# Six tiles instead of four in the second block group of a down projection

## The chip, the core and the metric

The kernel runs on one core of one Trainium2 chip. The metric is the device time of one execution in microseconds (us); the time of a kernel is the median of its runs. A time is compared only with one of the same chip.

## The reference: what is computed

The reference is a two-layer encoder over 1040 positions (16 learned tokens and 1024 frames) of width 1024. Each layer has an attention part (a gated linear attention group and a softmax group side by side) and a gated feed-forward part. The change lies in the last matrix product of the feed-forward part:

```python
def conv_ffn(x, w_up, conv_w, conv_b, w_down):
    h = x @ w_up
    ...
    u, g = jnp.split(hc, 2, axis=-1)
    return (jax.nn.silu(g) * u) @ w_down
...
        h = h + conv_ffn(rms_norm(h, ffn_norm[i]), w_up[i], conv_w[i], conv_b[i], w_down[i])
```

The inner width is 2816, that is 22 tiles of 128. So `@ w_down` sums 22 tiles into 8 output tiles of 128 rows, and the residual `h` is added to each. All data are 32-bit floats.

## The kernel before, in words

**Products.** TensorE multiplies in a one-pass 32-bit form. To keep the precision each operand is split into a high part (a cast on ScalarE) and a low part (a subtraction on VectorE), and each product is three matmuls: high x high, low x high, high x low (`mm3`, L257 to L263). A matmul covers 128 inner rows and, in layer 0, 260 columns (two pieces make a half of 520); in layer 1 the first 16 positions are no longer needed, and one piece of 512 makes a half.

**Groups.** The 22 inner tiles of the down projection are worked off in five groups (L52). The tuples name a kind, the first tile and the number of tiles: three plain tiles ("n"), a block group of eight ("s"), four plain tiles ("r"), a block group of four ("s"), and at the end `LAST`, three plain tiles that run in another routine (`down_last`), chunk by chunk, with the next norm.

- A plain group computes, for each output tile m and each half, the sum over its tiles in one PSUM tile; there are four of these (`p0` to `p3`), taken in turn. Kind "n" copies the PSUM tile by ScalarE into an SBUF tile "do" (L1718), and GpSimd stores that with an accumulating DMA onto the residual in DRAM, `hm` (L1720). Three "do" tiles go round. Kind "r" reads the residual `hm` back into eight tiles `hT` first (`load_residual`, L1688 to L1691, on SP's DMA queue) and adds the PSUM tile to them on VectorE (L1716).
- A block group (`down_blocks`, L1587) takes a product of two by two blocks with seven block products instead of eight (Strassen's scheme in the variant with fifteen additions). The blocks are a pair of output tiles (j = 0 to 3), the two halves of the group's inner tiles (nk each) and the two halves of the columns. A step of `seq` is one block product p = 1 to 7 of one pair j: nk x pieces x 3 matmuls, so there are 28 steps. The weight operands (the sums A21 + A22 and so on) are built per pair by `block_operand` (VectorE, L1147) and split by `up_split` (ScalarE L1165, VectorE L1166), four steps ahead of their use. The steps build two result tiles "du" and "dg" per pair, copied on ScalarE (L1626) and added to on VectorE (L1625). When one is complete, `hand_on` either adds it to `hT` on VectorE (L1617) if the residual has been read, or stores it with an accumulating DMA (L1620). In the kernel before, the first block group stores and the second one adds.

**Column operands.** `prepare` is a generator. Step by step it reads the stored activations back (`st`, L1490 and L1496, on SP's queue), builds the seven column operands of a block group (VectorE sums L1549, splits on ScalarE L377 and VectorE L378) and splits the tiles of a plain group (L1527, L1528). It works on up to four inner tiles at a time: `k0` = 0 takes two from each half; where nk is odd, the last turn takes one from each and its operands are half as wide. `pump` (L1580) runs some steps of it after each output tile of a plain group and at some steps of a block group, as long as enough slots are free. `complete` runs it on if something is needed and not there yet.

**Slots.** All these tiles lie in 39 SBUF slots of 1040 columns (33 and 6 of the feed-forward part), handed out from a list: a slot that is given back goes to its end, the next request takes from its front. A slot is given back in program order, so its next owner may have to wait for a store that still reads it. The "do" tiles are given back at the end of the plain group; "du" and "dg", where they are stored, four steps later (`LANDING`) or at the end of the group (L1666).

**Order.** On TensorE the program order is kept as written. On the other engines a planner sets the order from the program order and its own estimates, so loads and splits can move ahead of where the code has them; each engine then works its queue strictly in order. SP only issues DMAs: weight loads (L219 for plain tiles, L1132 for blocks), activation reads and the reads of the residual.

Of the kernel before, what the change touches and what calls it, by code (L numbers as in the profile page):

```python
# [23 lines left out]
T = META + SEQ  # L24
# [24 lines left out]

GROUPS, LAST = (("n", 0, 3), ("s", 3, 8), ("r", 11, 4), ("s", 15, 4)), (19, 3)  # L52
HALVES, HALVES_LAST, HALVES_OUT = (0, 520, 520), (8, 524, 516), (16, 528, 512)
AHEAD = 4
LANDING = 4
# [115 lines left out]
class Kern:  # L171
# [1412 lines left out]
            self.need = next(self.prep)  # L1584
            n -= 1

    def down_blocks(self, lyr, g0, ng, X, pp, fw, halves, after, hT):  # L1587


        nc, s = self.nc, self.slots  # L1590
# [21 lines left out]
        going = []  # L1612

        def hand_on(i, m, x):
            if hT:
                h = hT[m][:, o0:T]
                nc.vector.tensor_tensor(out=h, in0=x[:, o0:T], in1=h, op=ALU.add)  # L1617
                s.put(x)
            else:
                nc.gpsimd.dma_start(self.hm[m][:, o0:T], x[:, o0:T], accum_op=ALU.add)  # L1620
                going.append((i + LANDING, x))
# [26 lines left out]
        def run():  # L1648
            self.among_blocks = True
            for i, (j, p) in enumerate(seq):  # L1650
                ensure(i + AHEAD)
                q = st.setdefault(j, {})
                bank, begins = {2: "y", 5: "x", 3: "x"}.get(p, "a"), p in (1, 2, 5)
                if begins:
# [23 lines left out]
    def ffn_down(self, lyr, pp, fw, halves, acts, X, ids):  # L1678
# [6 lines left out]
        two = lambda ap: ap.rearrange("p (a b) -> p a b", b=n)  # L1685
        hT, ahead, going = [], [], []

        def load_residual():  # L1688
            for k in range(KD):
                hT.append(s.get(F32, f"h{k}", first=ids))  # L1690
                nc.sync.dma_start(hT[k][:, o0:T], self.hm[k][:, o0:T])  # L1691

# [7 lines left out]
        def plain(kind, g0, ng, m, w, nxt):  # L1700
            if m == 0:
                complete(lambda: all(j in acts for j in range(g0, g0 + ng)))
                if kind == "r" and not hT:
                    load_residual()
            if kind == "n" and m == 0:

                going.extend(s.get(F32, "do") for _ in range(3))
            out = hT[m] if kind == "r" else going[m % 3]
            for h in range(2):
                ps = pp.tile([128, 2, 512], F32, tag=f"p{(2 * m + h) % 4}", name="down", bufs=1)  # L1710
                for k in range(ng):
                    for c in range(pieces):
                        self.mm3(ps[:, c, :n], w[k], acts[g0 + k], halves[h] + c * n, n, k == 0, k == ng - 1)
                x = two(out[:, halves[h]:halves[h] + W])
                if kind == "r":
                    nc.vector.tensor_tensor(out=x, in0=ps[:, :pieces, :n], in1=x, op=ALU.add)  # L1716
                else:
                    nc.scalar.copy(x, ps[:, :pieces, :n])  # L1718
            if kind == "n":
                nc.gpsimd.dma_start(self.hm[m][:, o0:T], out[:, o0:T], accum_op=ALU.add)  # L1720
            if m == KD - 1:
                s.put(*going)
                going.clear()
                for j in range(g0, g0 + ng):
                    s.put(*acts.pop(j))
            if not (nxt and built(nxt)):
                self.pump(2)
# [17 lines left out]
        def run():  # L1745
            blocks = None
            for i, part in enumerate(parts):
# [5 lines left out]
                if nxt:  # L1753
                    then = parts[i + 2] if i + 2 < len(parts) else []
                    blocks = self.down_blocks(lyr, *nxt, X[nxt[0]], pp, fw, halves,
                                              lambda t=then: t and len(ahead) < 2 and fetch(t), hT)
                for k, t in enumerate(part):
                    for _ in range(2):
                        if len(ahead) < k + 3:
# [2 lines left out]
                        blocks[0](2 * (k - len(part) + 2) + 1)  # L1762
                    plain(*t, ahead[k], nxt)
                ahead.clear()
            if not hT:
                load_residual()
            complete(lambda: all(j in acts for j in range(LAST[0], sum(LAST))))
            return hT

# [183 lines left out]
```

## Time and profile before

| | |
|---|---|
| median of 3 runs | 2470.44 us (2469.42 to 2472.99) |
| the profiled execution | 2467.24 us |
| its span, first to last instruction | 2465.5 us |
| mean granted TensorE clock | 0.999 |
| DMA traffic over the span | 260.39 MB, mean 106 GB/s |
| accumulating stores of plain tiles (L1720) | 16, each 520 KB (512 in layer 1) |
| reads of the residual (L1691) | 16, each 520 KB (512 in layer 1) |

A page has the busy time of each engine with its share of the span (PE is TensorE's matmuls, PEld its weight loads, DVE VectorE, ACT ScalarE, POOL GpSimd; SP issues DMAs). A window row gives, for a stretch of the span, its length, each engine's busy time with the number of instructions, the granted clock in parts of full speed, the busy share of the 16 DMA engines and their rate. A row of the timeline has the start, the duration, the engine, the line, the operation, output and inputs, and in brackets the idle time of the engine before it and what ended that. A row of a tile has the shortest, median and longest duration in ns, and the first and the last start in us. In a row of grouped lines stand the busy time in us and the mean in ns, and the idle time before. A DMA queue's row has packets, megabytes, and the share of the 16 engines' time (q0 is GpSimd's queue of accumulating and other software DMAs, q1 SP's and ScalarE's); a row of DMA issues has the count, the size of one and the median time to landing. A row of waits has the total, the number and the longest.

### The profile page before, as it was taken

How to read it: one execution, taken by the hardware profiler on the slowest of the kernel's cores; microseconds unless marked ns; L12 is line 12 of the kernel's file. 1: busy time of each engine (PE TensorE's matmuls, PEld its weight loads, DVE VectorE, ACT ScalarE, POOL GpSimd, SP SyncE). 2: the span in 40 equal slices, each digit the busy share in tenths (PEclk: the TensorE clock that was granted, in tenths of full speed). 3: DMA queues.
4: the chain of work that ended last, by engine and by line, in shares of the span. 5: the costliest groups of instructions: out<-in, count | busy, mean ns of one | idle time of the engine just before them, and what ended most of it. 6: DMA issues, size and time to landing. Idle time of an engine off the chain costs nothing.

```text
span 2465.5 us, 47317 instructions
## 1 busy us (share of the span) xinstructions
PE 2437.9 (99%) x18286; PEld 2356.3 (96%) x18286; DVE 1876.9 (76%) x3769; ACT 1318.9 (53%) x2857; POOL 384.6 (16%) x565
## 2 busy tenths in 40 slices
PE   9999999999999999999999999999999999999998
PEld 8999999999999999999999999999999999997887
DVE  8666777769988888865966666777799888887567
ACT  7346666646555555642643566665465555556433
POOL 2023433210000000100210234331100000001002
PEclk9999999999999999999999999999999999999999
DMA  4222224343322214863312222243423212247822
GB/s 135 70 84 76 59 84 132 120 133 95 121 82 74 91 66 144 198 169 124 125 41 73 76 81 74 65 149 106 153 81 108 91 65 91 94 153 172 214 68 88
DMA packets 121680, 260.39 MB, mean 106 GB/s; under 512 B 15248, under 2 KB 37008, under 8 KB 121456
## 3 DMA queue, kind: packets, MB, share of 16 engines
q1 hardware_dynamic: 96864, 182.05, 23.9%
q0 software_dynamic: 22288, 72.81, 10.6%
q8 instruction: 143, 2.34, 0.4%
q10 hardware_dynamic: 2304, 2.52, 0.3%
q14 instruction: 81, 0.66, 0.1%
HBM read 176.74 MB, written 67.80 MB: 99 GB/s over the span
## 4 chain that ended last, share of the span: by engine, by line
PE 68%; issue 16%; DVE 10%; ACT 4%; DMA 1%; POOL 0%; SPq 0%; DVEq 0%; POOLq 0%; ACTq 0%
PE mm L261 8%; PE mm L263 8%; PE mm L262 8%; PE up L262 5%; PE up L263 5%; PE up L261 5%; PE down L262 5%; PE down L263 5%; PE down L261 5%; PE av L782 3%; PE tr L756 2%; PE S L720 1%; DVE S L723 1%; PE S L721 1%; ACT P L735 1%
## 5 line engine op out<-in xcount | busy, mean ns | idle before, releaser
L262 PE MATMUL up<-x,lo 128*128 128x260 f32 x2240 | 631.7, 282 | 1.0 <-DVE lo L1166 1.0
L261 PE MATMUL up<-x,hi 128*128 128x260 f32 x2240 | 631.9, 282 | 0.1
L263 PE MATMUL up<-x,hi 128*128 128x260 f32 x2240 | 631.6, 282 | 0.0
L262 PEld LDWEIGHTS up<-x,lo 128*128 128x128 f32 x2240 | 422.0, 188 | 1.5 <-DVE lo L1166 1.4
L261 PEld LDWEIGHTS up<-x,hi 128*128 128x128 f32 x2240 | 421.7, 188 | 0.4 <-ACT hi L1165 0.3
L263 PEld LDWEIGHTS up<-x,hi 128*128 128x128 f32 x2240 | 421.8, 188 | 0.0
L1165 ACT CAST hi<-raw 128x512 fp32r<-128x512 f32 (+1 forms) x490 | 266.5, 553 | 207.6 <-PE up L263 88.7
L261 PE MATMUL mm<-xh,hi 128*128 128x348 f32 (+6 forms) x1056 | 359.8, 341 | 0.0
L1166 DVE TENSOR_TENSOR lo<-raw,hi 128x512 fp32r<-128x512 f32 (+1 forms) x490 | 288.0, 603 | 79.7 <-ACT hi L1165 79.1
L263 PE MATMUL mm<-xl,hi 128*128 128x348 f32 (+6 forms) x1056 | 339.6, 322 | 0.0
L262 PE MATMUL mm<-xh,lo 128*128 128x348 f32 (+6 forms) x1056 | 338.6, 321 | 0.0
L261 PEld LDWEIGHTS mm<-xh,hi 128*128 128x128 f32 x1056 | 199.4, 189 | 2.3 <-issue 1.4
L262 PEld LDWEIGHTS mm<-xh,lo 128*128 128x128 f32 x1056 | 199.4, 189 | 0.3
L263 PEld LDWEIGHTS mm<-xl,hi 128*128 128x128 f32 x1056 | 198.6, 188 | 0.1
L1147 DVE TENSOR_TENSOR raw<-raw,raw 128x512 f32<-128x512 f32 (+1 forms) x230 | 147.5, 651 | 29.8 <-DMA raw<-in_wd_dram 27.5
L735 ACT ACTIVATE P<-S,m 116x460 f32<-116x460 f32 (+2 forms) x224 | 125.1, 562 | 77.5 <-DVE m L723 74.5
L228 ACT CAST hi<-raw 128x512 fp32r<-128x512 f32 (+2 forms) x152 | 87.4, 576 | 139.6 <-PE mm L263 56.2
L262 PE MATMUL down<-x,lo 128*128 128x260 f32 (+1 forms) x504 | 161.2, 320 | 0.2 <-DVE lo L1166 0.2
L263 PE MATMUL down<-x,hi 128*128 128x260 f32 (+1 forms) x504 | 161.0, 320 | 0.0
L261 PE MATMUL down<-x,hi 128*128 128x260 f32 (+1 forms) x504 | 161.0, 319 | 0.0
L378 DVE TENSOR_TENSOR PT<-tr,PT 116x464 fp32r<-116x464 f32 (+3 forms) x240 | 123.3, 516 | 48.9 <-ACT PT L377 47.2
L1427 POOL DMA_DIRECT2D actd<-cv x44 | 23.6, 537 | 734.6 <-DVE cv L1426 734.6
(313 smaller groups left out, 5957.4 us busy)
## 6 DMA issues: line engine op xcount, KB each, us to landing
raw<-in_wm_dram SPq DMA_DIRECT2D x326, 256.0 KB, 3.1
raw<-in_wd_dram SPq DMA_DIRECT2D x48, 256.0 KB, 4.2
actd<-cv POOLq DMA_DIRECT2D x22, 520.0 KB, 3.0
actd<-cv POOLq DMA_DIRECT2D x22, 512.0 KB, 3.0
cb<-cd SPq DMA_DIRECT2D x16, 520.0 KB, 3.8
kA<-kA SPq DMA_DIRECT2D x24, 260.0 KB, 4.1
kL<-kL SPq DMA_DIRECT2D x24, 260.0 KB, 4.7
st<-actd SPq DMA_DIRECT2D x24, 260.0 KB, 3.8
```

Source lines behind the costliest of these rows:

```text
L228: nc.scalar.copy(hi[:, :n, :], raw[:, :n, :])
L261: nc.tensor.matmul(ps, wh, xh[:, c0:c0 + n], start=first, stop=False, skip_group_check=more)
L262: nc.tensor.matmul(ps, wl, xh[:, c0:c0 + n], start=False, stop=False, skip_group_check=more)
L263: nc.tensor.matmul(ps, wh, xl[:, c0:c0 + n], start=False, stop=last, skip_group_check=more)
L378: nc.vector.tensor_tensor(out=lo, in0=src, in1=hi.bitcast(F32), op=ALU.subtract)
L720: nc.tensor.matmul(S[:rows, :n], q["qA"][e][:, qs], q["kA"][e][:, c0:k1], start=True, stop=False)
L735: nc.scalar.activation(P[:rows, :n], S[:rows, :n], AF.Exp, scale=-1.0, bias=m[:rows, nch - 1:nch], accum_out=(den if nch == 1 else d3[:row ...
L756: nc.tensor.transpose(tr[:w, 3 - j, :rows], P[:rows, o:o + w], id_)
L782: nc.tensor.matmul(av[:, a:b], w.rearrange("p a b -> p (a b)"), x, start=(t == ts[0] and part == 0 and i == 0), stop=(t == last and i == 1))
L1147: nc.vector.tensor_tensor(out=q[out][:, :nk, :], in0=q[a][:, :nk, :], in1=q[b][:, :nk, :], op=op)
L1165: nc.scalar.copy(hi[:, :nk, :], src[:, :nk, :])
L1166: nc.vector.tensor_tensor(out=lo[:, :nk, :], in0=src[:, :nk, :], in1=hi[:, :nk, :].bitcast(F32), op=ALU.subtract)
```

## The change

The four plain tiles and the block group of four become two plain tiles and a block group of six (nk = 3). The two plain tiles are of kind "n": ScalarE copies them out and GpSimd stores them with accumulating DMAs; kind "r" is gone. They use five "do" tiles in turn instead of three. The residual is no longer read ahead of the plain tiles, but inside the second block group, two tiles at each of the steps 1 to 4; `hand_on` then adds to them as before. The diff, without the lines that only hand the new argument through:

```diff
-GROUPS, LAST = (("n", 0, 3), ("s", 3, 8), ("r", 11, 4), ("s", 15, 4)), (19, 3)
+GROUPS, LAST = (("n", 0, 3), ("s", 3, 8), ("n", 11, 2), ("s", 13, 6)), (19, 3)
...
         def hand_on(i, m, x):
-            if hT:
-                h = hT[m][:, o0:T]
+            if residual:
+                h = residual[0][m][:, o0:T]
                 nc.vector.tensor_tensor(out=h, in0=x[:, o0:T], in1=h, op=ALU.add)
...
             for i, (j, p) in enumerate(seq):
                 ensure(i + AHEAD)
+                if residual and 1 <= i <= KD // 2:
+                    residual[1]((2 * i - 2, 2 * i - 1))
...
-        def load_residual():
-            for k in range(KD):
+        def load_residual(ks=range(KD)):
+            for k in ks:
                 hT.append(s.get(F32, f"h{k}", first=ids))
                 nc.sync.dma_start(hT[k][:, o0:T], self.hm[k][:, o0:T])
...
         def plain(kind, g0, ng, m, w, nxt):
             if m == 0:
                 complete(lambda: all(j in acts for j in range(g0, g0 + ng)))
-                if kind == "r" and not hT:
-                    load_residual()
             if kind == "n" and m == 0:
 
-                going.extend(s.get(F32, "do") for _ in range(3))
-            out = hT[m] if kind == "r" else going[m % 3]
+                going.extend(s.get(F32, "do") for _ in range(3 if ng > 2 else 5))
+            out = going[m % len(going)]
...
-                x = two(out[:, halves[h]:halves[h] + W])
-                if kind == "r":
-                    nc.vector.tensor_tensor(out=x, in0=ps[:, :pieces, :n], in1=x, op=ALU.add)
-                else:
-                    nc.scalar.copy(x, ps[:, :pieces, :n])
-            if kind == "n":
-                nc.gpsimd.dma_start(self.hm[m][:, o0:T], out[:, o0:T], accum_op=ALU.add)
+                nc.scalar.copy(two(out[:, halves[h]:halves[h] + W]), ps[:, :pieces, :n])
+            nc.gpsimd.dma_start(self.hm[m][:, o0:T], out[:, o0:T], accum_op=ALU.add)
...
                     blocks = self.down_blocks(lyr, *nxt, X[nxt[0]], pp, fw, halves,
-                                              lambda t=then: t and len(ahead) < 2 and fetch(t), hT)
+                                              lambda t=then: t and len(ahead) < 2 and fetch(t),
+                                              None if then else (hT, load_residual))
...
-            if not hT:
-                load_residual()
```

2 lines of the change are left out of this document (1 added, 1 removed).

## The prediction

> **What bounds the kernel now.** I read the page first, then one table of windows cut at the eight stages of the two down projections, then TensorE's waits, then the rows around the end of the first block group. The page says that TensorE is never free:
>
> ```profile
> span 2465.5 us, 47317 instructions
> PE 2437.9 (99%) x18286; PEld 2356.3 (96%) x18286; DVE 1876.9 (76%) x3769; ACT 1318.9 (53%) x2857; POOL 384.6 (16%) x565
> ```
>
> The windows are, for each layer, plain tiles 0 to 2, block group 3 to 10, plain tiles 11 to 14, block group 15 to 18:
>
> ```profile
> core 0: us, PE busy (x) PEld busy (x) DVE busy (x) ACT busy (x) POOL busy (x), PEclk, DMA share, GB/s
> 998.20:1032.70 34.50, 34.50 (x290) 34.50 (x289) 33.48 (x38) 27.86 (x40) 6.55 (x8) 1.00 0.83 177
> 1032.70:1113.30 80.60, 80.60 (x674) 80.60 (x673) 48.23 (x65) 34.02 (x53) 6.81 (x8) 1.00 0.72 193
> 1113.30:1159.60 46.30, 46.30 (x387) 46.30 (x386) 20.15 (x35) 6.45 (x12) 0.85 (x1) 1.00 0.40 118
> 1159.60:1199.80 40.20, 40.20 (x338) 40.20 (x337) 32.10 (x58) 22.29 (x48) 0.00 (x0) 1.00 0.20 57
> 2220.90:2255.40 34.50, 33.67 (x146) 27.00 (x145) 30.84 (x34) 26.70 (x39) 6.56 (x8) 1.00 0.80 178
> 2255.40:2333.80 78.40, 78.20 (x337) 63.00 (x336) 48.92 (x67) 34.48 (x54) 6.83 (x8) 1.00 0.74 194
> 2333.80:2378.30 44.50, 44.50 (x194) 36.01 (x193) 20.32 (x35) 5.89 (x11) 0.86 (x1) 1.00 0.41 122
> 2378.30:2417.20 38.90, 38.90 (x170) 31.54 (x169) 31.91 (x58) 22.16 (x48) 0.00 (x0) 1.00 0.20 55
> ```
>
> In the stages that change (third and fourth row of each layer) TensorE is busy for the whole window at clock 1.00. The others are not: VectorE has 20 of 46 us, ScalarE 6. And TensorE's list of waits has only these two in the whole down projection:
>
> ```profile
> PE down L261 <- ACT do L1718: 0.8, 1, 0.8
> PE down L262 <- DVE lo L1166: 0.2, 1, 0.2
> ```
>
> So the stages end when the matmuls end, and the change is worth its matmuls, less any new wait of TensorE.
>
> **Matmuls.** The code gives the counts (a window also catches two or three at its edges). A plain tile costs 8 outputs x 2 halves x 2 pieces x 3 = 96 matmuls in layer 0 and 48, twice as wide, in layer 1. A block group of 2 nk tiles costs 28 products x nk x 2 x 3 in layer 0, half in layer 1: 336 for nk = 2, 504 for nk = 3. The change removes two plain tiles and adds 168 block matmuls: 192 - 168 in layer 0, 96 - 84 in layer 1. Rates: plain 46.30/384 = 0.1206 us and block 40.20/336 = 0.1196 in layer 0; 44.50/192 = 0.2318 and 38.90/168 = 0.2315 in layer 1. Layer 0: 192 x 0.1206 - 168 x 0.1196 = 3.1 us less. Layer 1: 96 x 0.2318 - 84 x 0.2315 = 2.8 less. If the new nk = 3 products ran at the rate of the large group (80.60/672 = 0.1199, 78.40/336 = 0.2333) it would be 3.0 and 2.65. I take 5.7 for both.
>
> **Evacuation of the plain tiles.** From the queries on the tile "down" and on the operands:
>
> ```profile
> L1718 ACT COPY do<-down x32: 565/588/605, 1003.2 to 2256.7; 128x520 f32<-128x520 f32 x16, 128x512 f32<-128x512 f32 x16
> L1716 DVE TENSOR_TENSOR h<-down,h x32: 681/693/700, 1116.8 to 2378.5; 128x520 f32<-128x520 f32 x16, 128x512 f32<-128x512 f32 x16
> L377 ACT CAST x<-st x6: 1061/1063/1065, 1096.3 to 1120.6; 128x1040 fp32r<-128x1040 f32 x6
> L378 DVE TENSOR_TENSOR x<-st,x x6: 1231/1234/1243, 1100.5 to 1123.8; 128x1040 fp32r<-128x1040 f32 x6
> L1166 DVE TENSOR_TENSOR lo<-raw,hi 128x256 fp32r<-128x256 f32 x6 | 2.3, 416 | 0.0
> L228 ACT CAST wl<-raw 128x384 fp32r<-128x384 f32 x8 | 3.8, 520 | 0.9 <-PE down L262 0.9
> L230 DVE TENSOR_TENSOR wl<-raw,wl 128x384 fp32r<-128x384 f32 x5 | 2.7, 552 | 0.5 <-ACT wl L228 0.5
> ```
>
> Per layer 16 additions leave VectorE (16 x 0.693 = 11.1 us) and 16 copies come to ScalarE (16 x 0.588 = 9.4 us). The plain stage shrinks to 192 x 0.1206 = 23.1 us, one half-tile per 1.45 us. In it ScalarE has the 9.4 us, some two whole and seven half casts of block operands (2 x 1.06 + 7 x 0.6 = 6.3, the half cast taken from the copy of the same width), 8 weight casts (8 x 0.41, as L1166 of that width) and 4 of the next group (4 x 0.52): 21.1 of 23.1 us. VectorE: 3 x 1.23 + 11 x 0.69 for the operands, 8 x 0.42 and about 6 x 0.55 for weights: 17.9 us. Both fit, and the first plain stage shows TensorE full beside VectorE at 33.48 of 34.50 us. I cost this at nothing. The cover is the four PSUM tags: a copy may be some 4 x 1.45 - 1.45 = 4.3 us late; beyond that each us is one.
>
> In the second block group VectorE gets 28 x (0.552 - 0.416) = 3.8 us more for low parts and about 16 x 0.136 = 2.2 for sums, ScalarE 28 x 0.1 = 2.9, in a stage that grows from 40.2 to 60.3 us: nothing.
>
> **Accumulating stores and the later residual.** Each layer gets eight more accumulating stores from GpSimd, one each 2.89 us. The rows: the median landing of such stores (first) and of the residual reads (second), two DMA windows with these stores in both and hardware loads beside them, one with stores alone, and block-weight loads in the large group.
>
> ```profile
> DMA to landing us min/median/max: 5.6/7.5/10.0
> DMA to landing us min/median/max: 4.2/5.6/8.7
> q0 software_dynamic: 165, 0.62, 78.9%
> q1 hardware_dynamic: 165, 0.38, 27.5%
> q0 software_dynamic: 73, 0.24, 62.7%
> q1 hardware_dynamic: 95, 0.18, 39.7%
> q0 software_dynamic: 289, 1.05, 104.4%
> raw<-in_wd_dram SPq DMA_DIRECT2D x13, 256.0 KB, 4.9
> ```
>
> The third pair is 1116 to 1120 us, the next 2250 to 2252, the single 104.4% 2256 to 2262. Alone, 6 us at 104.4% moved 1.05 MB, two stores: 3.1 us of all DMA engines each. With loads beside them the stores have 62.7 to 78.9%: one each 3.1/0.789 = 4.0 to 3.1/0.627 = 5.0 us. That is slower than they are issued, so they queue. I take 4.0, as that window has the same neighbours. The last block store of the group before (POOL row below) is done by about 1121, so store m lands at 1121 + 4.0(m+1): 1125 for m = 0, 1153 for m = 7. The five "do" tiles make copy m = 5 (due 1129) wait for store 0, and m = 7 (due 1135) for store 2 (1133). Following the first-in-first-out list of slots through the code, the first "dg" tile of the next group (due 1147) gets the slot of store 3 (1137). None waits. On GpSimd the eight issues (0.86 us each, POOL rows below) find an empty queue.
>
> [...]
>
> The residual reads move from the plain stage into steps 1 to 4 of the group. SP issues in order, so a read that waits for its store holds all loads behind it. That happens today:
>
> ```profile
> 1120.59 0.32 SPq L1691 DMA_DIRECT2D h<-hm  x1
> 1121.01 0.38 SPq L219 DMA_DIRECT2D raw<-in_wd_dram  x1
> 1123.74 0.32 SPq L1691 DMA_DIRECT2D h<-hm  x1
> 1111.54 0.86 POOL L1620 DMA_DIRECT2D hm<-dg  x1 [9.25 <-ACT dg L1626]
> 1114.51 0.85 POOL L1620 DMA_DIRECT2D hm<-du  x1 [2.11 <-DVE du L1625]
> 1120.64 1.06 ACT L377 CAST x<-st 128x1040 fp32r<-128x1040 f32 x1 [6.81 <-DMA hm<-dg]
> ```
>
> After the change the last read goes at 1153, and behind it stand the weights of the third output pair, first used at step 12: 1136.4 + 12 x 2.15 = 1162.3 us. They need 4.9 us to land and 1.0 for the split, so SP must be free by 1156.4: 3.4 us to spare, and 1.6 in layer 1, where stage and steps are shorter (22.2 + 12 x 2.08 - 5.9 = 41.3 after the stage's start, against 39.7). The first additions of the residual come at step 6, with tiles 0 and 1, whose stores landed 20 us before. Cost: nothing, from 0 up to the rival's price.
>
> **Sum.** 0 - 5.7 us. Against the profiled execution (2467.24 us, of which the span is 2465.5) 2461.5; the median of the three runs is 3.2 us above it, so 2464.7 there. That is 0.23%, and 0.2% (4.9 us) is about what a measurement of this kernel can tell from no change: the margin is thin.
>
> **Rivals.** (B) ScalarE holds TensorE at the start of the plain stage. The last row above is ScalarE's in-order queue stopped for 6.81 us by an operand cast whose slot still feeds a block store; today no evacuation stands behind it. By the slot list the cast that gets this slot is now that of the second, half-wide operand 2, two casts later. If it is scheduled as early, ScalarE stands until 1120.6, its first copy ends at 1121.2, and TensorE needs that bank at 1113.3 + 4 x 1.45 = 1119.1: 2.1 us, in both layers 4.2. Result 2464.7 + 4.2 = 2468.9, and anything between. Against it: the residual reads that slowed that store are gone from there.
>
> (C) The stores back up far enough that SP comes free late and the third pair's weights stop TensorE. With p us per store the wait is 1121 + 8p - 1156.4 in layer 0, 1.8 more in layer 1: 16p - 69 together. It starts at p = 4.2, eats the gain at 4.7, and is slower by over 0.2% from 4.98; p = 5.2 gives 14.2 - 5.7 = 8.5 us more, 2479. For it: the 62.7% window, p = 5.0. Against it: the stores do not meet full neighbours all the time, and the loads of the reads spread out as the stores land. [...]
>
> (D) The change does not do what it says: the saved matmuls come back as a wait of the last three tiles, whose low weights now lie in slots of operand 2, free at step 25 of 28. That is 3 x 2.15 = 6.5 us ahead, against two operations of 0.55; it would have to slip by 5 us to matter. Result about 2470.
>
> **Chances.** Forecast 0.53, B 0.27, C 0.13, D 0.07. Of the forecast four fifths, and a tenth of B, lie beyond 4.9 us: faster 0.42 + 0.03 = 0.45. The rest of both and D is no change, 0.42; C is slower, 0.13. The range reaches from 2 us under the forecast (spread of the runs shown) through B: 2462.7 to 2470.2; outside are C and some of D.
>
> **What would show it.** Right: 36 matmuls fewer than 18286; third and fourth windows of each layer together 83.4 us instead of 86.5, and 80.6 instead of 83.4; no new wait of TensorE in "down". B shows as TensorE waiting for "do" copies behind a cast released by a store; C as TensorE waiting for "lo" near step 12, with SP stopped by residual reads; D as a wait for "wl". I am wrong if TensorE has over a microsecond of new waits, or if the stores land far past 10 us.

## The result and the profile after

The changed kernel takes 2500.43 us (median of four runs, 2498.55 to 2504.68) against 2471.6 us of the kernel before on the same chip: a ratio of 1.0125, interval 1.0114 to 1.0137. It is 28.8 us slower. The forecast was 2464.7 us and the range ended at 2470.2. Its profiled execution took 2501.63 us. The page of the changed kernel begins:

```profile
span 2499.8 us, 47317 instructions
...
PE 2444.4 (98%) x18250; PEld 2361.8 (94%) x18250; DVE 1873.3 (75%) x3755; ACT 1341.6 (54%) x2899; POOL 399.1 (16%) x581
```

The 36 matmuls are gone (18250 instead of 18286), and yet TensorE counts as busy for 6.5 us longer. The windows, cut at the first matmul of each stage (plain tiles and block group of layer 0, then of layer 1), show where the 34.3 us of span came from:

```profile
core 0: us, PE busy (x) PEld busy (x) DVE busy (x) ACT busy (x) POOL busy (x), PEclk, DMA share, GB/s
1116.10:1152.60 36.50, 26.60 (x194) 25.98 (x193) 14.47 (x26) 14.33 (x30) 6.83 (x8) 0.86 0.85 186
1152.60:1220.90 68.30, 62.15 (x506) 61.94 (x505) 36.18 (x55) 25.75 (x49) 0.85 (x1) 0.95 0.36 106
2354.70:2385.60 30.90, 24.31 (x97) 19.36 (x96) 13.99 (x26) 14.09 (x30) 6.39 (x8) 0.89 0.96 223
2385.60:2451.70 66.10, 60.40 (x254) 48.46 (x252) 36.13 (x56) 25.79 (x50) 1.29 (x2) 0.95 0.37 105
```

The prediction had 23.1 and 60.3 us for layer 0 and 22.2 and, at the same rate, 58.4 for layer 1, together 164.0. These rows add up to 201.8, so 37.8 us of new time; less the 5.7 us of matmuls saved, that is 32.1 of the 34.3; the other 2.2 us lie outside these rows and are not followed here. TensorE is idle for 9.9 us of the first row. The clock column has moved (1.00 in all eight rows before), and so has the DMA share of the plain stages, now 0.85 and 0.96. The four plain tiles before had 0.40, but over twice the length; over the same first 23.1 us they had 0.69:

```profile
1113.30:1136.40 23.10, 23.10 (x194) 23.10 (x193) 10.47 (x17) 3.36 (x5) 0.85 (x1) 1.00 0.69 208
```

So the DMA engines were well loaded before, and no load made TensorE wait. TensorE's waits in the down projection, of the changed kernel:

```profile
PE down L262 <- DVE lo L230: 15.0, 2, 8.4
PE down L261 <- DVE dg L1625: 12.5, 3, 6.2
...
PE down L261 <- ACT do L1714: 1.8, 2, 1.3
```

The first two stand for two long stops in each layer, one in the plain stage and one early in the block stage. Neither names a transfer, so one has to go back a step: what did VectorE do before that low part (L230 is the split of the plain weights)? Its timeline, of the changed kernel:

```profile
1130.72 0.42 DVE L230 TENSOR_TENSOR lo<-raw,hi 128x256 fp32r<-128x256 f32 x1
1142.25 1.49 DVE L1147 TENSOR_TENSOR raw<-raw,raw 128x384 f32<-128x384 f32 x3 [11.11 <-DMA raw<-in_wd_dram]
1143.66 0.42 DVE L230 TENSOR_TENSOR lo<-raw,hi 128x256 fp32r<-128x256 f32 x1
```

VectorE stood for 11.11 us because the next thing in its in-order queue was a weight sum of the block group to come (L1147), whose weights had not landed. The split that TensorE needed for the next-to-last output tile stood behind it. ScalarE stands for a load of the same kind, and the copy that would free a PSUM tile (L1714) stands behind it:

```profile
1146.92 0.93 ACT L1165 CAST hi<-raw 128x384 fp32r<-128x384 f32 x2 [13.29 <-DMA raw<-in_wd_dram]
1147.76 0.58 ACT L1714 COPY do<-down 128x520 f32<-128x520 f32 x1
```

And the weights come late. SP issued two of their loads at 1131.67 and 1132.2, with a residual read on either side; the planner had put the reads among the first pair's weights, not behind those of the first two pairs:

```profile
1131.25 0.33 SPq L1693 DMA_DIRECT2D h<-hm  x1
1131.67 0.93 SPq L1132 DMA_DIRECT2D raw<-in_wd_dram  x2
1134.15 0.33 SPq L1693 DMA_DIRECT2D h<-hm  x1
1144.11 0.33 SPq L1132 DMA_DIRECT2D raw<-in_wd_dram  x1
```

The two loads landed 10.6 and 13.1 us after their issue, and the first of them released VectorE. The load that released ScalarE is the third, of 1144.11, and that one was not slow: it landed in 2.8 us. It was issued late. SP's own waits, from 1115 to 1180 us, have the reason:

```profile
SPq L1132 <- DVE lo L230: 12.5, 2, 9.6
```

Weight loads of plain tiles and blocks share a ring of four buffers. SP stood 9.6 us for one that VectorE's split L230 gave back at the end of the third row of its timeline above, and this split stood behind the late sum. So one late load stops VectorE, and through the full ring also SP, the next load and ScalarE. No run has more than four buffers, so what the ring adds to the loss is not known.

The time from issue to landing of the weight loads between 1125 and 1170 us, in the kernel before (loads of 128 KB) and then in the changed one (192 KB; without the new stores such loads landed in 2.3 to 2.4 us at the median, see the experiments):

```profile
DMA to landing us min/median/max: 2.0/2.1/4.1
```

```profile
DMA to landing us min/median/max: 2.3/5.0/13.1
```

What moved beside them, in the changed kernel from 1128 to 1147 us (q0 has the accumulating stores, q1 the loads and reads):

```profile
q0 software_dynamic: 706, 2.60, 72.0%
q1 hardware_dynamic: 805, 1.97, 31.0%
```

The last thing to see is behind each long stop. Windows of the changed kernel, first the stop and then what follows it, twice:

```profile
1135.40:1144.10 8.70, 0.30 (x3) 0.09 (x1) 1.83 (x4) 0.00 (x0) 0.00 (x0) 0.76 1.05 252
1144.10:1150.10 6.00, 5.96 (x27) 5.96 (x28) 3.04 (x7) 3.17 (x8) 0.56 (x1) 0.50 0.65 219
...
1167.50:1174.00 6.50, 0.35 (x4) 0.14 (x3) 2.81 (x6) 1.00 (x2) 0.00 (x0) 0.75 0.39 152
1174.00:1177.60 3.60, 3.60 (x17) 3.60 (x18) 3.10 (x5) 0.00 (x0) 0.00 (x0) 0.51 0.40 109
```

After a stop of 8.7 us TensorE ran 6.0 us at clock 0.50: 27 matmuls where 50 would fit, 3.0 us lost on top. The five stops of the two layers, from matmul to matmul, are 1.6, 8.7, 6.4, 7.0 and 6.1 us (29.8), and the four long ones are followed by 6.0, 3.6, 4.0 and 3.6 us at half clock (8.6 lost): 38.4 together, close to the 37.8 us of the windows.

### The profile page after: what moved, and what is told of

It is laid out like the page before. It is cut to its first block, busy times and chain, and to the rows that moved or that the text cites. A ratio compares the mean times of both kernels' runs of the same rounds, so it can differ in the third digit from the quotient of the medians.

```text
span 2499.8 us, 47317 instructions
## 1 busy us (share of the span) xinstructions
PE 2444.4 (98%) x18250; PEld 2361.8 (94%) x18250; DVE 1873.3 (75%) x3755; ACT 1341.6 (54%) x2899; POOL 399.1 (16%) x581
## 5 line engine op out<-in xcount | busy, mean ns | idle before, releaser
L1165 ACT CAST hi<-raw 128x512 fp32r<-128x512 f32 (+2 forms) x490 | 272.9, 565 | 222.8 <-PE up L263 89.4
L1166 DVE TENSOR_TENSOR lo<-raw,hi 128x512 fp32r<-128x512 f32 (+2 forms) x490 | 295.7, 616 | 92.3 <-ACT hi L1165 91.2
L1147 DVE TENSOR_TENSOR raw<-raw,raw 128x512 f32<-128x512 f32 (+1 forms) x230 | 151.8, 668 | 69.4 <-DMA raw<-in_wd_dram 66.9
L261 PE MATMUL down<-x,hi 128*128 128x260 f32 (+1 forms) x588 | 189.8, 323 | 12.5 <-DVE dg L1625 12.5
L262 PE MATMUL down<-x,lo 128*128 128x260 f32 (+1 forms) x588 | 189.4, 322 | 0.0
L263 PE MATMUL down<-x,hi 128*128 128x260 f32 (+1 forms) x588 | 189.1, 322 | 0.0
L228 ACT CAST hi<-raw 128x512 fp32r<-128x512 f32 (+3 forms) x152 | 84.1, 554 | 108.0 <-PE mm L263 54.9
```

What stands on the lines that cost most here:

```text
L228: nc.scalar.copy(hi[:, :n, :], raw[:, :n, :])
L261: nc.tensor.matmul(ps, wh, xh[:, c0:c0 + n], start=first, stop=False, skip_group_check=more)
L262: nc.tensor.matmul(ps, wl, xh[:, c0:c0 + n], start=False, stop=False, skip_group_check=more)
L263: nc.tensor.matmul(ps, wh, xl[:, c0:c0 + n], start=False, stop=last, skip_group_check=more)
L1147: nc.vector.tensor_tensor(out=q[out][:, :nk, :], in0=q[a][:, :nk, :], in1=q[b][:, :nk, :], op=op)
L1165: nc.scalar.copy(hi[:, :nk, :], src[:, :nk, :])
```

## The experiments

The theories, as the expectations name them. T1: residual reads that wait for their stores hold SP, and the weights behind them are late. T2: the accumulating stores load the DMA engines, and so the weights land late, whatever the order. T3: the block group of six itself is too much for operands built four steps ahead. T4: the order of the queues (weight operands ahead of the evacuation) and the late loads together. T5: that order alone. Ratios are to the kernel before, on the same chip, with 95% intervals.

**The sizes alone.** The kernel before with groups of two and six; nothing else of the change (the two plain tiles are of kind "r", and the residual is read ahead of them).

```diff
-GROUPS, LAST = (("n", 0, 3), ("s", 3, 8), ("r", 11, 4), ("s", 15, 4)), (19, 3)
+GROUPS, LAST = (("n", 0, 3), ("s", 3, 8), ("r", 11, 2), ("s", 13, 6)), (19, 3)
```

> The kernel before with two plain tiles of kind r (residual read ahead of them, VectorE adds) and the block group of six: the sizes alone, no extra accumulating stores, no later read. Theory T1 (the later residual reads wait in SP's in-order queue for the plain stores and hold the block weights behind them; VectorE's queue then stops in front of TensorE's operands): the reads wait only for the first group's stores, as before, so most of the matmul gain comes: 2464 to 2469 us against some 2471 before. T2 (the eight accumulating stores take the DMA engines, so weights land late in whatever order they are issued): also 2464 to 2469, there are none. T3 (the nk = 3 group itself is short of lookahead, since only nk = 2 loads its next pair early): TensorE waits 6 us near the seventh step of the group in each layer as in the changed kernel, 2478 to 2484.

2472.86 us, ratio 1.0013 (1.0004 to 1.0022). That is outside all three ranges. The block stages took 60.3 and 58.4 us at full clock, so T3 falls. The plain stages lost more than the matmuls saved: 30.9 and 26.0 us instead of 23.1 and 22.2. The gaps lie behind VectorE's additions to the residual, which wait for the reads; the first, of 1.6 us, lies behind an operand split whose slot still feeds a block store (TensorE's waits, then VectorE's from 1114 to 1146 us, split first):

```profile
PE down L261 <- DVE h L1716: 6.8, 3, 3.6
```

```profile
DVE x L378 <- DMA hm<-dg: 4.2, 1, 4.2
DVE h L1716 <- DMA h<-hm: 3.1, 1, 3.1
```

So the sizes without the rest of the change are worth nothing either: the reads come too late for a plain stage of two tiles.

**Residual reads on GpSimd's queue.** The changed kernel; GpSimd's queue has nothing else in the block stage, and SP keeps the weights to itself.

```diff
-                nc.sync.dma_start(hT[k][:, o0:T], self.hm[k][:, o0:T])
+                self.tc.keep_in_program_order(nc.gpsimd.dma_start(hT[k][:, o0:T], self.hm[k][:, o0:T]))
```

> The changed kernel with the residual reads issued by GpSimd, kept behind the plain stores in its queue; SP has no read that waits. Stores, sizes and DMA traffic stay. T1: both waits of TensorE (8.7 and 6.4 us in layer 0) go, 2464 to 2472. T2: they stay, since the stores still share the DMA engines with the weights, 2490 to 2500. T3: the first goes and the second, in the block group, stays: 2478 to 2484.

2485.13 us, 1.0057 (1.004 to 1.0075): half of the loss, and between the ranges of T2 and T3. The stop early in the block stage shrinks to 1.7 us. The one in the plain stage stays, with 5.8 us in layer 0 (8.7 before this edit) and 5.1 in layer 1, now behind ScalarE, which still waits for the late weights (TensorE's waits, then ScalarE's from 1115 to 1185 us):

```profile
PE down L261 <- ACT do L1714: 14.1, 7, 5.5
```

```profile
ACT hi L1165 <- DMA raw<-in_wd_dram: 9.7, 1, 9.7
```

**Reads that wait for no store.** The changed kernel; the reads take the same bytes from the scratch of the activations, so what is added to the output is not the residual.

```diff
-                nc.sync.dma_start(hT[k][:, o0:T], self.hm[k][:, o0:T])
+                nc.sync.dma_start(hT[k][:, o0:T], self.actd[k][:, o0:T])
```

> The changed kernel with the residual reads taken from the stored activations of tiles 0 to 7 (so the sum that is added is not the residual): same bytes, same SP queue, no read waits for a plain store, except for a slot. T1: most of the loss goes, 2464 to 2475. T2: the loss stays, 2490 to 2500. T3: the second wait stays, 2478 to 2484.

2501.79 us, 1.013 (1.0115 to 1.0146), as slow as the change, where T2 had 2490 to 2500. So T1 is not needed for the loss: up to 1141 us SP waits for none of these stores, and the block weights that it issued until then took 8.8 to 13.9 us to land. (Later it still waits for some, whose slots it needs.) That T1 has no part in the changed kernel does not follow, since the reads now go earlier (five of them by 1134 us, two in the changed kernel) and load the DMA engines there (share 0.99 to 1.06 from 1129 to 1141.2 us). The weight loads are later still, median 8.4 us where the changed kernel has 5.0:

```profile
DMA to landing us min/median/max: 2.9/8.4/13.9
```

**Reads in the order of the code.** The changed kernel with the reads kept on SP where the code issues them (what the prediction had assumed).

```diff
-                nc.sync.dma_start(hT[k][:, o0:T], self.hm[k][:, o0:T])
+                self.tc.keep_in_program_order(nc.sync.dma_start(hT[k][:, o0:T], self.hm[k][:, o0:T]))
```

> The changed kernel with the residual reads held in program order on SP, so that the planner cannot move them ahead of the first two pairs' weights: the order that the prediction had assumed. T1: the first wait (plain stage, 8.7 us and the slow matmuls after it) goes; the second stays or grows, because the third pair's weights and the second pair's other blocks stand behind reads that wait for the last stores: 2480 to 2488. T2: 2492 to 2500. The prediction's own arithmetic (the reads cost nothing in this order): 2465.

2493.54 us, 1.0094 (1.0079 to 1.0109), in T2's range. By the two ratios 7 to 8 of the 29 us hang on the planner's order; with the assumed one the prediction would have been wrong all the same. TensorE's longest wait is again for the copies:

```profile
PE down L261 <- ACT do L1714: 13.6, 6, 5.5
```

**Without the plain tiles' stores.** Reads on GpSimd as above, and the accumulating stores of the two plain tiles left out, so that what these tiles add is missing in the output.

```diff
-            nc.gpsimd.dma_start(self.hm[m][:, o0:T], out[:, o0:T], accum_op=ALU.add)
+            if ng > 2:
+                nc.gpsimd.dma_start(self.hm[m][:, o0:T], out[:, o0:T], accum_op=ALU.add)
```

> The changed kernel with the residual reads on GpSimd's queue (as in the run that gave 2485), and without the accumulating stores of the two plain tiles between the groups (16 of them are gone; what those two tiles add to the output is left out). The order of ScalarE's, VectorE's and SP's queues around the plain stage should stay about as it was. Theory T4 (the hoisted weight operands stand in front of the evacuation AND their loads land late because the stores hold the DMA engines): without the stores the loads land in about 2 to 3 us, the waits of ScalarE's first block cast (9.66 us there) and of VectorE's block sum (7.21) fall below 4 us, TensorE's gap of 5.8 us goes, 2464 to 2470 us. Rival T5 (the order of the queues alone, whatever the traffic): the gap of 5 to 6 us stays in both layers, 2480 us or more. Rival T2 (the stores' traffic alone, whatever the order) also expects 2464 to 2470; the next run tells T2 from T4.

2465.4 us, 0.9982 (0.9972 to 0.9991). Without the stores the stages are what the prediction had, at clock 1.00 (windows of this run, layer 0), and the loads land as before:

```profile
1116.90:1140.00 23.10, 23.10 (x195) 23.10 (x193) 14.49 (x26) 14.33 (x30) 4.59 (x8) 1.00 0.72 191
1140.00:1200.30 60.30, 60.30 (x506) 60.30 (x505) 36.03 (x55) 25.76 (x49) 0.53 (x1) 1.00 0.26 89
```

```profile
DMA to landing us min/median/max: 2.3/2.4/8.0
```

The clean pair is this run and the one with the reads on GpSimd: 0.9982 and 1.0057, with nothing but the stores between them. T5 falls: ScalarE's first block cast still stands ahead of plain copies (it waits 1.85 us), and this order alone costs nothing when the loads are on time.

**Block operands in the order of the code.** The changed kernel, with the first sums, casts and splits of the block group kept where the code issues them (`pin` is set around the call that builds them ahead, for the second group).

```diff
+    def pinned(self, ins):
+        if self.pin:
+            self.tc.keep_in_program_order(ins)
...
-            nc.vector.tensor_tensor(out=q[out][:, :nk, :], in0=q[a][:, :nk, :], in1=q[b][:, :nk, :], op=op)
+            self.pinned(nc.vector.tensor_tensor(out=q[out][:, :nk, :], in0=q[a][:, :nk, :], in1=q[b][:, :nk, :], op=op))
...
+                        self.pin = not then
                         blocks[0](2 * (k - len(part) + 2) + 1)
+                        self.pin = False
```

> The changed kernel, with the second group's first weight sums on VectorE and their casts and splits kept in the order in which the code issues them, so that all plain weights' low splits stand ahead of the block sums on VectorE, and four of the last copies on ScalarE ahead of the first block cast but two more behind it. SP still has the residual reads among the weights. T4: the gaps in the plain stage (8.7 and 7.0 us, with the half clock behind them) shrink to 3 us or less, but the block stage still begins with late weights (6 us): 2482 to 2490. T2 (traffic alone): nothing changes, 2498 to 2503. T5 (order alone): 2475 to 2485.

2490.36 us, 1.0083 (1.0068 to 1.0098). Ten us less than the change, just above what T4 gave (2482 to 2490), and not by its mechanism: the long stop of the plain stage did not shrink, it moved to the end of that stage (9.5 us at 1142.2, 8.8 at 2373.3), behind copies that still have a block cast ahead of them, and the one in the block stage fell to 1.8 us.

```profile
PE down L262 <- ACT do L1719: 21.1, 6, 9.2
```

**Slots given back later.** The changed kernel; this is rival B alone.

```diff
-                while going and (going[0][0] <= i or i == len(seq) - 1):
+                while going and going[0][0] <= i:
...
                     for held, _, _ in X.pop(p):
                         s.put(*held)
+                    if i == len(seq) - 1:
+                        s.put(*(x for _, x in going))
```

> The changed kernel, with the first block group's last stored slots given back behind the operand slots instead of ahead of them, so that the casts at the start of the plain stage take slots that no store still reads. This is the prediction's rival B alone. T4 and B together: only the first gap of the plain stage (1.6 us + 0.4 us in layer 0) goes, 2496 to 2500. If B were the start of the whole chain (the late copies making everything behind them late), the gaps of 8.7 and 7.0 us shrink too: below 2490.

2498.65 us, 1.0109 (1.0094 to 1.0125). The edit did not take the wait away: a later cast gets such a slot instead and waits as long, 5.5 us where the changed kernel has 5.3. The first gap stays, at 1.8 us. So this run does not price B.

```profile
ACT x L377 <- DMA hm<-dg: 5.5, 1, 5.5
```

**All three together** (reads on GpSimd, operands in code order, slots later).

> All three together: residual reads on GpSimd's queue, block operands in code order, slots given back later. T4: no gap of TensorE over 3 us in the plain stage or at the start of the block stage, 2464 to 2475; the prediction's sum without its rivals was 2464.7. T2 (the stores' traffic alone): the loads are as late as with the reads on GpSimd alone, 2480 to 2487.

2486.12 us, 1.0057 (1.0041 to 1.0074): no better than the reads on GpSimd alone, and in T2's range. T4 falls in its strong form, and T2 stands. The plain stage is nearly whole, and the late loads now hold the block stage, 70.3 instead of 60.3 us (windows of this run, layer 0):

```profile
1118.30:1144.00 25.70, 23.56 (x194) 23.14 (x192) 9.86 (x18) 12.35 (x26) 5.96 (x7) 1.00 0.91 179
1144.00:1214.30 70.30, 63.29 (x504) 62.98 (x505) 41.46 (x68) 27.72 (x54) 5.95 (x10) 0.93 0.43 135
```

The order of the queues decides where the late weights hurt, not whether.

**Reads spread over the block stage.** All three together, but the reads on SP in code order, each pair some steps ahead of its use.

```diff
-                if residual and 1 <= i <= KD // 2:
-                    residual[1]((2 * i - 2, 2 * i - 1))
+                if residual and i in (1, 6, 13, 18):
+                    c = (1, 6, 13, 18).index(i)
+                    residual[1]((2 * c, 2 * c + 1))
```

> As the run with all three together (2486), but the residual reads stay on SP's queue in the code's order, and each pair of tiles is read a few steps before its own tiles are handed on (steps 1, 6, 13 and 18 of the block stage) instead of all eight within steps 1 to 4. The same bytes move. In the run with all three, the second pair's weights landed 8.1 us after issue (median) beside a burst of eight reads, and TensorE stood 7.3 and 8.3 us in the block stage. If the DMA engines' load at that place is the cause: those gaps fall below 3 us, 2468 to 2476. If it is the stores alone that make the weights late, or the ring of four weight buffers: 2482 to 2488.

2483.76 us, 1.0063 (1.0048 to 1.0078). That is in the range of the second alternative, the stores alone or the ring of four weight buffers. The stops are 5.7 us, and 4.4 us at the end of layer 1's plain stage. SP's timeline shows one read before the first pair's weights were all issued and three more ahead of the second pair's. It shows the ring too: between 1128 and 1150 us SP waited 8.7 us for a buffer that VectorE's sum gives back, and the load at 1143.45 comes behind that wait. Reads, stores and ring are not separated by this run.

```profile
1134.24 0.46 SPq L1701 DMA_DIRECT2D h<-hm  x1
1143.45 0.33 SPq L1133 DMA_DIRECT2D raw<-in_wd_dram  x1
1148.50 1.33 SPq L1701 DMA_DIRECT2D h<-hm  x3
1149.94 2.15 SPq L1133 DMA_DIRECT2D raw<-in_wd_dram  x3
```

```profile
SPq L1133 <- DVE raw L1148: 8.7, 1, 8.7
```

**No reads.** All three together without the residual reads; each tile is doubled by the same VectorE instruction, and the residual is left out of the output.

```diff
-                self.tc.keep_in_program_order(nc.gpsimd.dma_start(hT[k][:, o0:T], self.hm[k][:, o0:T]))
...
-                nc.vector.tensor_tensor(out=h, in0=x[:, o0:T], in1=h, op=ALU.add)
+                nc.vector.tensor_tensor(out=h, in0=x[:, o0:T], in1=x[:, o0:T], op=ALU.add)
```

> As the run with all three together (2486), without the residual reads at all (each tile is doubled by the same VectorE instruction instead of having the residual added, so the residual is left out of the output). The accumulating stores of the plain tiles remain. With the run without those stores (2465.4, reads there) it makes a square. If stores and reads together overload the DMA engines: 2463 to 2470. If the stores alone do it: 2480 or more. If each costs a part: between.

2473.23 us, 1.0021 (1.0012 to 1.0031): between, so each costs a part. With stores and reads the ratio was 1.0057, with stores alone 1.0021, with reads alone 0.9982 (this last one without the edits to the slots and the operands' order; the two runs with stores and reads, with and without these edits, are both at 1.0057). Taking the reads away gives 0.36%, some 9 us; taking the stores away gives 0.75%, some 18.5 us. The median landing does not rank the runs: it is 8.1 us here, with 0.21% lost, and 5.0 in the changed kernel, with 1.25%. What counts is which load is late and what stands behind it. In layer 1 the stores alone fill the DMA engines for the whole plain stage (share 1.02), and the block stage behind takes 63.7 us instead of 58.4:

```profile
2335.30:2357.50 22.20, 22.20 (x97) 18.00 (x96) 10.73 (x19) 12.54 (x26) 6.26 (x8) 1.00 1.02 203
2357.50:2421.20 63.70, 60.35 (x253) 48.42 (x253) 39.91 (x66) 27.23 (x53) 1.40 (x2) 0.97 0.32 82
```

**The sizes alone, mended.** The first experiment with the slots given back later, and then with the reads on GpSimd as well (edits as above).

> Not the change itself but what its sizes could be worth: the kernel before with groups of two and six tiles (residual added in place, no new stores; 2472.9 with TensorE gaps of 1.6, 3.9 and 2.3 us), and the first group's last stored slots given back behind the operand slots. If the 1.6 us come from VectorE waiting for such a slot and the other gaps follow from it: 2464 to 2468, faster than both. If they come from SP, which issues the reads only at 1121.7 us: 2470 to 2474.

> The previous run with the residual reads on GpSimd's queue, where nothing stands behind them in this stage. If SP's queue was what held them: no gap over 1 us in the plain stage of either layer, 2463 to 2467, faster than both kernels. If eight reads in a burst make the plain weights late: gaps of some 3 us at the third or fourth tile, 2470 to 2476.

2475.05 us, 1.0026 (1.0017 to 1.0035), just above both ranges, and 2475.89 us, 1.0032 (1.002 to 1.0045), in the range for late weights, though the weights were on time (median 2.4 us). Neither pays. With the slots the first gap goes and one of 3.4 us per layer is left. With GpSimd there is one of 4.3 and one of 3.8 us, and SP's queue is not what held the reads. On GpSimd's own timeline the first two go at 1116.54, right behind the last store of the block group before, and the gap in layer 0 (1119.5 to 1123.8) ends with their landing and VectorE's additions. The third read also waits 3.83 us for the landing of such a store.

```profile
1116.54 1.32 POOL L1693 DMA_DIRECT2D h<-hm  x2
1121.69 3.13 POOL L1693 DMA_DIRECT2D h<-hm  x6 [3.83 <-DMA hm<-du]
```

**Half the bytes.** If the traffic is the cause, the same sizes with less of it should give the matmuls' gain. ScalarE copies the plain tiles straight into the residual's tiles, nothing is stored, and once a block tile has been added, one accumulating load brings the residual in. The full computation, with eight accumulating transfers per layer over the whole block stage in place of eight stores and eight reads. The slots are given back later, as above, and the reads at the start of the block stage are gone.

```diff
                 nc.vector.tensor_tensor(out=h, in0=x[:, o0:T], in1=h, op=ALU.add)
+                nc.gpsimd.dma_start(h, self.hm[m][:, o0:T], accum_op=ALU.add)
                 s.put(x)
...
-            out = going[m % len(going)]
+            if ng == 2:
+                hT.append(s.get(F32, f"h{m}", first=ids))
+            out = going[m % 3] if ng > 2 else hT[m]
...
-            nc.gpsimd.dma_start(self.hm[m][:, o0:T], out[:, o0:T], accum_op=ALU.add)
+            if ng > 2:
+                nc.gpsimd.dma_start(self.hm[m][:, o0:T], out[:, o0:T], accum_op=ALU.add)
```

> The sizes of the change with half its DMA bytes: the two plain tiles are copied by ScalarE straight into the residual's eight SBUF tiles and not stored, and after a block tile has been added to such a tile, GpSimd issues one accumulating load of the residual into it; so there are eight accumulating transfers per layer, spread over the block stage, and no residual reads. Slots are given back behind the operands. Theory (the 30 us came from the DMA engines' load at the plain stage, the rest from the slot's wait): the weights land in 2 to 3 us, no gap of TensorE over 3 us, and the time is the prediction's sum without its rivals, 2464.7, to that sum with the slot's wait (2.1 us per layer), 2469; faster than before or the same. If the eight accumulating transfers make the weights late wherever they lie: 2475 to 2485.

> The previous run without the later giving back of the slots. If the slot's wait costs about 2 us per layer here as in the changed kernel: 2 to 4 us above the previous run. If the order of the slots does nothing, as it did in the changed kernel: within 2 us of it.

2467.41 us, 0.999 (0.9981 to 0.9999), and with the slots as before 2469.32, 1.0001 (0.9992 to 1.0009). The medians differ by 1.9 us, between "within 2" and "2 to 4", and the two intervals just overlap, so the slots' order is not shown to matter. The edit changes number, bytes and place of the transfers together, so these are not told apart. The stages are those of the sum, and the loads are on time (windows, then landings between 1125 and 1170 us, of the first of the two):

```profile
1114.30:1137.40 23.10, 23.10 (x195) 23.10 (x194) 13.86 (x27) 14.10 (x29) 0.84 (x1) 1.00 0.56 133
1137.40:1197.80 60.40, 60.40 (x507) 60.40 (x506) 36.46 (x55) 25.55 (x49) 5.19 (x6) 1.00 0.44 93
1197.80:1247.90 50.10, 47.09 (x282) 45.57 (x281) 40.33 (x65) 27.77 (x60) 26.34 (x30) 1.00 0.56 169
```

```profile
DMA to landing us min/median/max: 2.2/2.3/5.9
```

The third row is the stage behind, 45.9 us in the kernel before: 4.2 us of the gain are given back there. In the last run the last pair's two loads are issued at step 15 instead of at the end.

```diff
+                if residual and i == 15:
+                    for m in (KD - 2, KD - 1):
+                        self.tc.keep_in_program_order(
+                            nc.gpsimd.dma_start(residual[0][m][:, o0:T], self.hm[m][:, o0:T], accum_op=ALU.add))
```

> The run that accumulates the residual into the eight tiles (2467.4), with the last pair's two accumulating loads issued at step 15 of the block stage instead of after the pair is handed on at its end. In that run the two stages came out as the prediction's sum has them (23.1 and 60.4 us), but layer 0's next stage took 50.2 us instead of 45.9, with TensorE gaps of 0.7 to 1.7 us behind VectorE's additions. If the late landing of the last pair's loads causes this: that stage falls to 46 to 47 us and the time to 2463 to 2465. If it is the order of VectorE's queue in that stage, which this edit leaves as it was: 50 us and 2466 to 2469.

2465.44 us, 0.9988 (0.9979 to 0.9997), and that stage is down from 50.1 to 46.7 us:

```profile
1198.50:1245.20 46.70, 46.08 (x282) 45.38 (x281) 39.05 (x65) 27.75 (x60) 24.33 (x28) 1.00 0.49 159
```

So the last pair's late loads caused most of that stage's extra time. The ratio itself, 0.9988 against 0.9990 on another chip, does not show a gain over the run before. This version computes the whole reference; it is faster than the changed kernel, and 0.12% faster than the kernel before.

## Why the prediction was wrong, point by point

- **What bounds the kernel now** holds. "The change is worth its matmuls, less any new wait" is how the result came out; the new waits, with the slow matmuls behind them, are 38 us.
- **Matmuls** was right. 36 fewer ran, and in the four runs with the plain stores left out or replaced by accumulating loads the stages took 23.1 and 60.3 to 60.4 us in layer 0, 22.2 to 22.4 and 58.4 to 58.5 in layer 1, as the sum had them.
- **Accumulating stores and the later residual** is the step that failed: "None waits" and "Cost: nothing". It worked out when the stores land and who waits for a store. It did not ask when the loads beside them land: it priced a block-weight load at 4.9 us, and only for the third pair. The first pair's loads took 10.6 and 13.1 us. With the stores left out the whole loss is gone (ratio 0.9982, where the same kernel with them has 1.0057); with the waits for them in the plain stage taken away (reads that wait for no store) nothing is. The residual reads have a part too: in the runs with all three edits, 0.36% of a loss of 0.57% goes with them. The price of a store was right: by the queue rows above 2.60 MB of stores in 19 us, 3.9 us for each of 520 KB, where the prediction had 4.0. "None waits" held for the copies, which had no wait for a plain store; SP's reads, though, waited for such stores five times, 17.8 us in all, the longest 5.3. The lines for the question were there: the DMA rates quoted from the large group were of loads and stores that share the engines. With 3.1 us of all engines per store, eight need 25 us in a plain stage of 23.1.
- **The place of the reads**, within the same step, was wrong too: the prediction had only the third pair's weights behind them, and the planner put them among the first pair's. That is worth 7 to 8 us (ratios 1.0125 and 1.0094), no more.
- **Evacuation of the plain tiles**, "I cost this at nothing", failed through its cover. The 4.3 us of PSUM may well be right; ScalarE's busy time of 21.1 us counted the "4 of the next group" as work only. They are also places in an in-order queue where 13.3 us of waiting in layer 0 and 11.5 in layer 1 came to stand ahead of the copies. Before the change ScalarE had none of this evacuation behind them.
- **Rival B** was right in size, 1.6 us against 2.1, in layer 0 only. In the changed kernel ScalarE stood 5.3 us until 1123.64 for the slot of a block store, as B has it. The new stores did not hold it up: the first of them was issued at 1125.05. In the other runs that keep these stores it was 5.2 to 5.5 us, but 2.4 in one (reads that wait for no store); in the run without them it was 2.2. So why it is as long as it is stays open. The edit meant to remove it alone moved it to another cast; it is gone (or down to 0.5 us) only in the runs with accumulating loads, where the traffic is gone too.
- **Rival C** had the right kind, late weights behind the stores, but the wrong place (third pair instead of the first and second). That SP held by reads is the path is not shown: freed of waiting for stores in the plain stage the reads cost as much (ratio 1.013), moved to GpSimd they cost half, which may as well be because they go later there.
- **Rival D** did not appear: no wait for "wl" in "down".
- Missing from the sum was the **clock**: 8.6 of the 38 us were lost to half speed (0.50 to 0.51) behind the stops.

The chance given to a slowdown, 0.13, hung on one path. What stays open is how the DMA engines divide themselves between a store, a read and a weight load; the runs show the total, not the rule. In the queue rows of the changed kernel the two queues moved about as many packets (706 and 805), and those of the stores took more than twice the engines' time (72.0 against 31.0%); no run tests what sets these shares.

## What to carry to other kernels

When a change adds transfers, price the lateness of the loads that share the engines, not only the landing of the new ones: here 25 us of stores in a 23 us stage, with the residual reads, took weight loads from 2.4 to 5.0 us at the median and 13 at worst. When a copy moves to another engine, list what stands ahead of it in that in-order queue and what each of these waits for; reordering only moved such a wait here. And look for the form with fewer bytes first: accumulating into SBUF once replaced a store and a read, and turned a loss of 1.2% into a small gain.

## What the runs showed of the hardware

In all eight rows of the down projection before, TensorE's clock was 1.00. In the changed kernel each of the four long stops (8.7, 6.4, 7.0 and 6.1 us) was followed by 3.6 to 6.0 us at clock 0.50 or 0.51, so each cost 1.8 to 3.0 us more than itself. Its stop of 1.6 us was not: the row from 1116.1 to 1135.4 us, which has that stop in it, is at 1.00. The sizes alone had stops of 1.6, 3.9 and 2.3 us, and a lower clock behind the last two (windows of that run, each stop and then what follows it):

```profile
1122.00:1123.80 1.80, 0.47 (x4) 0.27 (x3) 1.80 (x3) 0.77 (x2) 0.00 (x0) 1.00 0.98 206
1123.80:1127.90 4.10, 4.10 (x35) 4.10 (x36) 4.08 (x8) 0.76 (x3) 0.00 (x0) 1.00 0.90 298
1127.90:1131.80 3.90, 0.33 (x4) 0.14 (x2) 0.86 (x2) 0.74 (x3) 0.00 (x0) 0.82 0.38 147
1131.80:1136.00 4.20, 4.20 (x19) 4.20 (x20) 4.20 (x9) 0.63 (x1) 0.00 (x0) 0.50 0.47 142
...
2346.10:2348.60 2.50, 0.62 (x3) 0.19 (x3) 2.05 (x3) 0.75 (x2) 0.00 (x0) 1.00 0.97 202
2348.60:2352.60 4.00, 4.00 (x11) 3.15 (x12) 4.00 (x8) 1.10 (x3) 0.00 (x0) 0.57 0.88 296
```

With the reads that wait for no store, a row of 2.0 us with TensorE busy for 0.26 was followed by 4.0 us at 0.59, and one of 3.2 us with 0.41 busy by 2.6 us at 1.00. So these rows show no single length of stop from which on the clock falls.

The weight loads that SP issued between 1125 and 1170 us landed in 2.3 to 2.4 us at the median in six runs without the stores of the two plain tiles, and in 3.6 to 8.4 us in the nine with them (5.0 in the changed kernel).
